# Nineteen pairs of projection units a layer as seven half-size products, gates through DRAM, units in 272 columns

## The chip, the cores and the metric

The kernel is one program on one core of a Trainium2 chip. The metric is the device time of one execution, in microseconds (us). The engines named below are TensorE (PE; its weight loads are PEld), VectorE (DVE), ScalarE (ACT), GpSimd (POOL) and SyncE (SP), which issues most of the DMAs.

## The reference, cut to what matters

Two layers of a trunk run over 1024 prompt tokens and 64 sample tokens (T = 1088 columns), with a model width of 1024. In each layer one projection of the normed input feeds four token mixers and the gates of the merge:

```python
h = rmsnorm(x, norm_w[l])
proj = h @ w_in[l]                       # 1024 -> 11,792 columns
(a_x, a_b, a_c, a_z, s_u, s_z, c_q, c_f, c_i, c_z,
 d_q, d_k, d_v, d_z, d_r, m_logit) = jnp.split(proj, pts, axis=-1)
...                                      # A short conv, B S5, C HGRN2, D GLA
branches = jnp.stack([y_a, y_b, y_c, y_d], axis=2)      # 512 channels each
p = jnp.einsum('blnw,nwd->blnd', branches, w_branch[l])
gates = jax.nn.sigmoid(m_logit.reshape(bsz, L, N_BRANCH, D_MODEL))
merged = jnp.sum(gates * p, axis=2)
x = x + merged @ w_out[l]
```

All of it is float32; the final output is normed once more.

## The kernel before

**Tiles.** Channels lie on the partitions and the 1088 tokens on the free axis. The normed input `h` is eight k-tiles of [128, 1088], each held as a high and a low part in float32r (`split`: ScalarE copies the high part, VectorE subtracts it). Weights come as tiles of [128, 4, 128] (four k-tiles by 128 output channels, 256 KB) and are split in the same way by `w_split`: `whi` by ScalarE, `wlo` by VectorE. A product is three matmuls: high x high, high x low, low x high.

**Units.** `unit(KT, xs)` makes 128 output channels for all tokens: for each k-tile, for each of the three parts, three matmuls of 384, 384 and 320 columns into one PSUM tile of three banks (`mm`, two such tiles). Projections have KT = 8; the branch outputs and the half-GLU have KT = 4. `tokens_unit` makes the values of the recurrences with the tokens on the partitions. The first two units of a layer (`lead_units`) take the tokens a third at a time.

**Order.** `ORDER` lists the units of a layer: S5 inputs (u), convolution (A: four units each), HGRN heads (H), GLA pairs (G), S5 outputs and half-GLU (U). `merge` follows: for each of four branches eight gate units (KT = 8, then a sigmoid by ScalarE) and eight branch units (KT = 4), with the product gate x branch on VectorE and the sum on GpSimd. `out_proj` closes the layer. Beside the stream of units run "lanes" (`Lane`, `pump`, `drain`): chains of small stages for the recurrences, S5 and setup, which are issued where a rough account of the engines (`Book`) finds their operands ready. `drain` issues what is left of a lane at once. `defer` holds small steps of which one is issued per k-step. Every engine's queue runs in the order of issue.

**Memory.** There are `NBIG` = 38 slots of [128, 1088]. `h` takes 16 of them from the lead units until the last gate unit of the merge. The lines of the profile all read L81: one helper (`Meter`) passes every instruction on, so rows are told apart by tile names (`mm` a unit's PSUM, `sm` a lane's).

## Time and profile before

| | |
|---|---|
| time, median of three runs | 3117.66 us (3117.42 to 3119.92) |
| the profiled execution: its span | 3116.5 us; the median of the runs is 1.2 us above it |
| TensorE busy | 3074.3 us in 19650 matmuls |
| VectorE, ScalarE, GpSimd busy | 1482.8, 969.4, 477.0 us |
| moved by DMA | 215.30 MB, 69 GB/s |
| instructions | 47347 |

The span is from the first to the last instruction. Busy time counts an engine's instructions where they overlap once only; a matmul's own duration overlaps with the next one's, so the cost of one in a stream is the step from one start to the next.

### The profile page before, as it was taken

The numbers are of one execution on the slowest core, as the hardware profiler recorded it, in microseconds if no ns is written. First come the engines' busy times: TensorE is split into PE (matmuls) and PEld (weight loads), VectorE is DVE, ScalarE is ACT, GpSimd is POOL, SyncE is SP. The second block draws the span as 40 slices with busy tenths as digits, with TensorE's granted clock in tenths as the row PEclk, the third lists the DMA queues.
The fourth block names the chain that finished last, engine by engine and source line by source line (L and its number), as shares of the span: only waits on it lengthen the run. The fifth ranks groups of instructions, "written<-read, shape, count | busy, mean of one in ns | idle before, by whom it ended". The sixth has DMA issues, their size and how long they took to land.

```text
span 3116.5 us, 47347 instructions
## 1 busy us (share of the span) xinstructions
PE 3074.3 (99%) x19650; PEld 2977.8 (96%) x19650; DVE 1482.8 (48%) x2670; ACT 969.4 (31%) x1769; POOL 477.0 (15%) x490
## 2 busy tenths in 40 slices
PE   8999999999999999999999999999999999999998
PEld 7999989999999999999899999999999999999997
DVE  4688665465641222116446885555565412221152
ACT  5223333425451212113331233334255412111221
POOL 2323011020210011103013411010202001111020
PEclk9999999999999999999999999999999999999999
DMA  4223122112331221213232221221113321212222
GB/s 133 71 69 95 36 59 75 36 36 62 82 110 44 73 73 45 73 45 98 85 90 82 75 71 58 60 64 36 39 54 80 113 73 45 73 48 70 58 85 88
DMA packets 260491, 215.30 MB, mean 69 GB/s; under 512 B 13984, under 2 KB 238000, under 8 KB 260276
## 3 DMA queue, kind: packets, MB, share of 16 engines
q1 hardware_dynamic: 251908, 185.14, 21.0%
q0 software_dynamic: 8368, 27.13, 2.7%
q8 instruction: 155, 2.54, 0.3%
q14 instruction: 60, 0.49, 0.1%
HBM read 168.14 MB, written 44.08 MB: 68 GB/s over the span
## 4 chain that ended last, share of the span: by engine, by line
PE 91%; DVE 4%; ACT 2%; issue 1%; POOL 1%; DMA 0%; SPq 0%; DVEq 0%; POOLq 0%; ACTq 0%
PE mm L81 79%; PE sm L81 12%; POOL mg L81 1%; ACT hi L81 0%; DVE att L81 0%; DVE wlo L81 0%; DVE g L81 0%; DVE prs L81 0%; DVE lo L81 0%; DVE H L81 0%; DVE w L81 0%; DVE pr L81 0%; DVE ya L81 0%; ACT L81 0%; ACT whi L81 0%
## 5 line engine op out<-in xcount | busy, mean ns | idle before, releaser
L81 DVE TENSOR_TENSOR wlo<-wraw,whi 128x512 fp32r<-128x512 f32 x400 | 298.5, 750 | 762.3 <-ACT whi L81 761.6
L81 PE MATMUL mm<-hi,wlo 128*128 128x384 f32 (+1 forms) x2592 | 580.7, 330 | 0.0
L81 PE MATMUL mm<-lo,whi 128*128 128x384 f32 (+1 forms) x2592 | 580.0, 330 | 0.0
L81 PE MATMUL mm<-hi,whi 128*128 128x384 f32 (+1 forms) x2592 | 576.7, 329 | 2.2 <-DVE g L81 1.0
L81 ACT ACTIVATE whi<-wraw 128x512 fp32r<-128x512 f32 x400 | 275.5, 692 | 741.8 <-PE mm L81 651.8
L81 PEld LDWEIGHTS mm<-hi,whi 128*128 128x128 f32 x2592 | 440.7, 188 | 5.5 <-issue 2.8
L81 PEld LDWEIGHTS mm<-hi,wlo 128*128 128x128 f32 x2592 | 442.3, 188 | 1.6 <-issue 1.3
L81 PEld LDWEIGHTS mm<-lo,whi 128*128 128x128 f32 x2592 | 441.0, 189 | 2.2 <-issue 1.6
L81 PE MATMUL mm<-xh,wlo 128*128 128x384 f32 (+1 forms) x1920 | 433.9, 331 | 1.2 <-DVE wlo L81 1.2
L81 PE MATMUL mm<-xh,whi 128*128 128x384 f32 (+1 forms) x1920 | 433.8, 331 | 1.0 <-ACT whi L81 0.8
L81 PE MATMUL mm<-xl,whi 128*128 128x384 f32 (+1 forms) x1920 | 433.1, 331 | 0.0
L81 PEld LDWEIGHTS mm<-xh,wlo 128*128 128x128 f32 x1920 | 328.3, 189 | 5.1 <-DVE wlo L81 2.8
L81 PEld LDWEIGHTS mm<-xh,whi 128*128 128x128 f32 x1920 | 328.1, 189 | 4.7 <-issue 1.9
L81 PEld LDWEIGHTS mm<-xl,whi 128*128 128x128 f32 x1920 | 327.8, 190 | 1.9 <-issue 1.5
L81 POOL TENSOR_TENSOR mg<-mg,g 128x1088 f32<-128x1088 f32 x46 | 136.8, 2974 | 1004.3 <-DVE g L81 974.2
L81 ACT ACTIVATE g<-mm 128x768 f32<-128x768 f32 (+1 forms) x128 | 72.9, 621 | 335.7 <-PE mm L81 335.7
L81 DVE TENSOR_TENSOR g<-g,mm 128x768 f32<-128x768 f32 x96 | 64.8, 716 | 122.3 <-PE mm L81 122.3
L81 ACT ACT_TABLE_LOAD x90 | 115.5, 1283 | 14.4 <-PE mm L81 12.1
L81 DVE COPY_PREDICATED att<-mask,sm 64x32 f32<-64x32 int32 (+9 forms) x184 | 93.7, 568 | 32.1 <-PE sm L81 31.8
L81 PE MATMUL mm<-hi,hi 128*128 128x512 f32 x256 | 79.3, 391 | 5.1 <-DVE g L81 3.2
L81 POOL DMA_DIRECT2D out_dram<-S x24 | 18.0, 751 | 430.2 <-DVE S L81 362.9
L81 PEld LDWEIGHTS sm<-q,k 128*64 128x64 f32 (+5 forms) x800 | 80.4, 172 | 2.9 <-issue 1.3
(332 smaller groups left out, 3996.9 us busy)
## 6 DMA issues: line engine op xcount, KB each, us to landing
wraw<-in_w_in_dram SPq DMA_DIRECT2D x328, 256.0 KB
y<-ysc SPq DMA_DIRECT2D x32, 544.0 KB
wraw<-in_w_branch_dram SPq DMA_DIRECT2D x64, 256.0 KB
ysc<-o POOLq DMA_DIRECT2D x16, 544.0 KB, 3.1
wo<-in_w_out_dram SPq DMA_DIRECT2D x16, 512.0 KB
out_dram<-S POOLq DMA_DIRECT2D x12, 512.0 KB, 4.6
usc<-u SPq DMA_DIRECT2D x8, 544.0 KB
ysc<-ya SPq DMA_DIRECT2D x8, 544.0 KB
```

The source lines that it names most:

```text
L81: r = fn(*a, **kw)
```

## The change

- 38 of a layer's 76 eight-tile units become 19 pairs (`PAIRED`): the convolution's (A: x with c, b with z), the S5 output gates (Z) and 18 of the 32 merge gates (M). A pair is a product of a 256-channel weight block with `h`, both cut in halves along the reduction, and the tokens cut in halves of 544: seven products of quarter blocks in place of eight (Strassen, in Winograd's form). `combine` makes the sums of quarters of `h` once a layer and splits them into high and low parts (16 slots); `prep` makes the sums of weight tiles on VectorE ahead of each split; `pair` runs the products and puts the results together out of PSUM on VectorE.
- All merge gates are computed ahead of the merge, the other 14 by `gate_unit`, stored to DRAM (`gsc`) and loaded by `merge`, which now has branch units alone, in the order 0, 2, 1, 3. The S5 output gates go through DRAM too (`szs`).
- Units run in two halves of 544 tokens, each two matmuls of 272 columns; `mm` is two banks in three buffers, and each half is emptied by itself (`out`).
- S5 of a layer (its loads too) starts after the pairs; the setup of S5 is drained after the third unit; the half-GLU's loads and gelus are issued beside the last GLA gate unit (`glu_begin`). Half of the merge's sums move from GpSimd to VectorE.
- Weight tiles have six buffers for raw loads, filled by `feed`, and the scratch of software-issued DMAs is 4096 bytes.

```diff
-ORDER = 'u0 u1 u2 u3 A0 A1 A2 H0 H1 H2 H3 G0 G1 A3 U'
+PAIRED = 'A0 M0 A1 M1 A2 M2 A3 M3 Z0 M4 Z1 M5 M6 M7 M8'
+EARLY = 'm18 m19'
+ORDER = 'm20 m21 m22 m23 m24 m25 m26 m27 m28 m29 m30 m31 H0 H1 H2 H3 G0 G1 U'
+BRANCHES = (0, 2, 1, 3)
+RAWS = 6
...
-        return self.ps.tile([128, 3, 512], F32, tag="mm", name=self.nm("mm"))
+        return self.ps.tile([128, 2, 512], F32, tag="mm", name=self.nm("mm"), bufs=3)
...
+    def feed(self):
+        while self.di in self.loaded:
+            self.di += 1
+        if self.nraw < RAWS:
+            self.w_dma(self.di)
+    def prep(self, j):
+        if j >= len(self.seq) or j in self.done:
             return
+        self.done.add(j)
         nc = self.nc
+        e, p = self.seq[j]
+        perm = self.plan[e][2]
+        drop = []
+        for i in range(e, e + (1 if p is None else 4)):
+            self.w_dma(i)
+        if p is None:
+            src = self.raws[e]
+            drop = [e]
+        else:
+            a11, a21, a22, a12 = (self.raws.get(e + i) for i in range(4))
+            new = lambda: self.wp.tile([128, 4, 128], F32, tag="wsum", name=self.nm("wsum"), bufs=2)
+            if p == 0:
+                src = a11
+            elif p == 1:
+                s1 = new()
+                src = new()
+                self.sums_[e] = s1, src
+                nc.vector.tensor_add(s1[:], a21[:], a22[:])
+                nc.vector.tensor_sub(src[:], s1[:], a11[:])
+            elif p == 2:
+                src = a12
+            elif p == 3:
+                src = self.sums_[e][0]
+            elif p == 4:
+                src = a21
+                nc.vector.tensor_sub(a21[:], a11[:], a21[:])
+                drop = [e, e + 1]
+            elif p == 5:
+                src = self.sums_.pop(e)[1]
+                nc.vector.tensor_sub(src[:], a12[:], src[:])
+                drop = [e + 3]
+            else:
+                src = a22
+                drop = [e + 2]
         hi = self.wp.tile([128, 4, 128], F32R, tag="whi", name=self.nm("whi"), bufs=4)
         lo = self.wp.tile([128, 4, 128], F32R, tag="wlo", name=self.nm("wlo"), bufs=4)
+        h, lv, r = hi[:], lo[:], src[:]
...
         nc.scalar.activation(h, r, AF.Copy)
         nc.vector.tensor_sub(lv, r, h.bitcast(F32))
+        for i in drop:
+            self.raws.pop(i)
+            self.nraw -= 1
+        self.ws[j] = (hi, lo)
+    def unit(self, KT, xs, out, last=False):
         nc = self.nc
+        j0, nw = self.wi, KT // 4
+        self.prep_to(j0 + nw)
+        ws = [self.ws.pop(j0 + i) for i in range(nw)]
+        self.wi += nw
+        for hb in range(2):
+            ps = self.mm()
+            for k in range(KT):
+                hi, lo = ws[k // 4]
+                xh, xl = xs[k]
+                terms = ((hi, xh), (hi, xl), (lo, xh))
+                for j, (wt, xt) in enumerate(terms):
+                    for b in range(2):
+                        s = HT * hb + HP * b
+                        nc.tensor.matmul(ps[:, b, :HP], wt[:, k % 4, :], xt[:, s:s + HP],
+                                         start=(k == 0 and j == 0), stop=(k == KT - 1 and j == len(terms) - 1))
+                    if j + 1 < len(terms):
+                        self.pump()
+                if k == 1:
+                    self.prep_to(self.wi + 1 + hb + (KT < 8))
+                if k % 4 == 2:
+                    self.feed()
+                if k % 2:
+                    self.step()
+                else:
                     self.pump()
+            out(ps[:, 0:2, :HP], (HT * hb, HT), 2)
+    def combine(self):
+        nc = self.nc
+        xs = [[None] * 4 for _ in range(4)]
+        f = {}
+        def full(i):
+            for n in (i, i + 4):
+                f[n] = self.big([128, T], name="xf")
+                (nc.gpsimd if n > 3 else nc.vector).tensor_add(f[n], self.h[n][0].bitcast(F32), self.h[n][1].bitcast(F32))
+        def sums(i):
+            a, b = f[i], f[i + 4]
+            t = self.big([128, 2, HT], name="xd")
+            f[i, 0] = t
+            nc.vector.tensor_sub(t[:, 1], b[:, HT:T], a[:, HT:T])
+            nc.vector.tensor_sub(t[:, 0], a[:, HT:T], a[:, 0:HT])
+            nc.vector.tensor_add(a[:, 0:HT], t[:, 1], a[:, 0:HT])
+            nc.vector.tensor_sub(b[:, 0:HT], b[:, 0:HT], a[:, 0:HT])
+        def split(i, n):
+            src = (f[i][:, 0:HT], f[i, 0][:, 0], f[i, 0][:, 1], f[i + 4][:, 0:HT])[n]
+            x = self.big([128, 2, HT], F32R, name="xc")
+            nc.scalar.activation(x[:, 0], src, AF.Copy)
+            nc.vector.tensor_sub(x[:, 1], src, x[:, 0].bitcast(F32))
+            xs[n][i] = (x[:, 0], x[:, 1])
+            if n == 3:
+                self.free(f[i], f[i + 4], f[i, 0])
+        self.h_sums = xs
+        for i in range(4):
+            self.defer.append(lambda i=i: full(i))
+            self.defer.append(lambda i=i: sums(i))
+            self.defer.append(lambda i=i: (split(i, 0), split(i, 1)))
+            self.defer.append(lambda i=i: (split(i, 2), split(i, 3)))
+    def quarters(self):
+        q = lambda k0, s: [tuple(x[:, s:s + HT] for x in self.h[k0 + k]) for k in range(4)]
+        t2, t1, t3, t4 = self.h_sums
+        return q(0, 0), t2, q(4, 0), t1, t3, q(4, HT), t4
+    def pair(self, out, a, b):
+        nc = self.nc
+        V = None
+        two = lambda x: x.rearrange("p (b n) -> p b n", b=2)
+        H1, H2 = slice(0, HT), slice(HT, T)
+        ops = self.quarters()
+        ps = {}
+        for p in range(7):
+            self.prep_to(self.wi + 1)
+            hi, lo = self.ws.pop(self.wi)
+            self.wi += 1
+            at, start = ((0, True), (1, True), (0, False), (2, True), (3, True), (2, False), (3, False))[p]
+            if start:
+                ps[at] = self.mm()
+            for k in range(4):
+                xh, xl = ops[p][k]
+                for j, (wt, xt) in enumerate(((hi, xh), (hi, xl), (lo, xh))):
+                    for c in range(2):
+                        nc.tensor.matmul(ps[at][:, c, :HP], wt[:, k, :], xt[:, HP * c:HP * c + HP],
+                                         start=(start and k == 0 and j == 0), stop=(k == 3 and j == 2),
+                                         skip_group_check=True)
+                    if j < 2:
+                        self.pump()
+                if k == 1:
+                    self.prep_to(self.wi + 3)
+                if k == 2:
+                    self.feed()
+                self.step()
+            v = ps[at][:, 0:2, :HP]
+            if p == 0:
+                V = self.big([128, HT], name="V")
+                nc.scalar.copy(two(V), v)
+            elif p == 1:
+                nc.vector.tensor_add(two(V), two(V), v)
+            elif p == 2:
+                out(0, v)
+            elif p == 3:
+                nc.vector.tensor_add(two(b[:, H2]), two(V), v)
+            elif p == 4:
+                nc.vector.tensor_add(two(b[:, H2]), two(b[:, H2]), v)
+            elif p == 5:
+                nc.vector.tensor_add(two(a[:, H2]), two(V), v)
+                out(1, None)
+            else:
+                nc.vector.tensor_add(two(b[:, H1]), two(V), v)
+                self.free(V)
+                out(2, None)
+    def pair_of(self, f, g, names=("pa", "pb")):
+        nc = self.nc
+        a, b = (self.big([128, T], name=n) for n in names)
+        two = lambda x: x.rearrange("p (b n) -> p b n", b=2)
+        def out(i, v):
+            if i == 0:
+                nc.scalar.activation(two(a[:, 0:HT]), v, f)
+            elif i == 1 and f != AF.Copy:
+                nc.scalar.activation(a[:, HT:T], a[:, HT:T], f)
+            elif i == 2 and g != AF.Copy:
+                nc.scalar.activation(b, b, g)
+        self.pair(out, a, b)
+        return a, b
...
+    def gate_unit(self, l, i):
+        g = self.big([128, T], name="g")
+        self.proj(l, "g", i, self.evac(g, AF.Sigmoid))
+        self.nc.sync.dma_start(self.gsc[l][i // 8][128 * (i % 8):128 * (i % 8) + 128, :], g)
+        self.free(g)
+    def gates_pair(self, l, j):
+        pair = self.pair_of(AF.Sigmoid, AF.Sigmoid, ("ga", "gb"))
+        for i, t in enumerate(pair):
+            d = 2 * (j % 4) + i
+            self.nc.sync.dma_start(self.gsc[l][j // 4][128 * d:128 * d + 128, :], t)
+            self.free(t)
+    def glu_begin(self, l):
...
+        for j in range(4):
+            load(j)
+        self.defer += [lambda: None] * YLAG
+        for j in range(4):
+            self.defer.append(lambda j=j: act(j))
...
+        u, ac = self.pair_of(AF.Copy, AF.Copy, ("au", "ac"))
+        nc.vector.tensor_mul(u, u, ac)
+        self.free(ac)
...
+        b, z = self.pair_of(AF.Copy, AF.Silu, ("ab", "az"))
+        nc.vector.tensor_mul(y, y, b)
         nc.vector.tensor_mul(y, y, z)
+        self.free(b)
...
+        units = [(n, d) for n in BRANCHES for d in range(8)]
+        g = {}
+        def gate(i):
+            if i < len(units):
+                n, d = units[i]
+                g[i] = self.big([128, T], name="g")
+                nc.sync.dma_start(g[i], self.gsc[l][n][128 * d:128 * d + 128, :])
+        def branch(i, y):
+            n, d = units[i]
+            gi = g.pop(i)
+            first = n == BRANCHES[0]
...
+            def out(p, span, nb):
+                gv = self.cut(gi, span, nb)
+                nc.vector.tensor_mul(self.cut(md, span, nb) if first else gv, gv, p)
+                if not first:
+                    s = slice(span[0], span[0] + span[1])
+                    (nc.vector if span[0] else nc.gpsimd).tensor_add(md[:, s], md[:, s], gi[:, s])
+            self.unit(4, y, out, last=(d == 7))
+            self.free(gi)
+        y = self.y
+        gate(0)
+        gate(1)
+        for i, (n, d) in enumerate(units):
+            b = i // 8
+            if d == 0 and b:
+                while self.defer:
+                    self.defer.pop(0)()
+                y = nxt
+            if d == 5 and b < 3:
+                if b == 2:
+                    self.drain(self.rec)
+                    self.drain(self.aux)
+                nxt = self.load_y(l, BRANCHES[b + 1])
+                self.defer += [lambda: None] * 4 + [lambda y=nxt, j=j: self.split(y, j) for j in range(4)]
...
+            gate(i + 2)
+            branch(i, y)
...
     def layer(self, l):
         if l:
-            self.s5l.q.append(self.s5_load(l))
             self.lead_units(l, lambda b, k: self.drain(self.aux) if b == 2 and k == 0 else None,
                             lambda b, k: self.step())
         self.aux.q.append(self.conv_begin(l))
+        if l:
+            self.keep = 0
+            self.combine()
+        self.u_unit(l, 2)
+        if l == 0:
+            self.drain(self.s5l)
+            self.keep = 0
+            self.combine()
+        self.u_unit(l, 3)
+        for op in EARLY.split():
+            self.gate_unit(l, int(op[1:]))
+        for op in PAIRED.split():
+            while self.defer:
+                self.defer.pop(0)()
+            self.drain(self.aux)
+            {"A": self.conv, "Z": self.z_pair, "M": self.gates_pair}[op[0]](l, int(op[1:]))
...
+        self.aux.q.append(self.conv_end(l))
+        self.s5l.q.append(self.s5_load(l))
         self.s5l.q.append(self.s5(l))
+        self.more = True
         for op in ORDER.split():
             i = int(op[1:] or 0)
-            if op[0] == "u":
-                if i > 1:
-                    self.u_unit(l, i)
-            elif op[0] == "A":
-                self.drain(self.aux)
-                self.conv(l, i)
-            elif op[0] == "H":
+            if op[0] == "H":
                 self.hgrn_units(l, i)
+            elif op[0] == "m":
+                self.gate_unit(l, i)
             elif op[0] == "G":
                 self.gla_units(l, i)
             else:
-                self.drain(self.tabs)
-                self.drain(self.s5l)
                 self.glu(l)
-        self.aux.q.append(self.conv_end(l))
...
+    nc = _bacc.Bacc("TRN2", target_bir_lowering=False, num_devices=1, dynamic_dma_scratch_size=4096)
```

## Rows read from the trace of the kernel before

**Rows 1.** The page: busy time of TensorE, and its granted clock in slices.
```profile
PE 3074.3 (99%) x19650; PEld 2977.8 (96%) x19650; DVE 1482.8 (48%) x2670; ACT 969.4 (31%) x1769; POOL 477.0 (15%) x490
...
PEclk9999999999999999999999999999999999999999
```

**Rows 2.** The page: the chain that ended last, by engine.
```profile
PE 91%; DVE 4%; ACT 2%; issue 1%; POOL 1%; DMA 0%; SPq 0%; DVEq 0%; POOLq 0%; ACTq 0%
```

**Rows 3.** The same chain in time (start us, us, what): longest piece.
```profile
2437.58 572.72 PE mm L81 x3450
```

**Rows 4.** Timeline of PE (start us, us), values unit: its longest wait.
```profile
398.65 0.58 PE L81 MATMUL mm<-whi,xh 128*128 128x256 f32 x1 [5.77 <-ACT v L81]
```

**Rows 5.** Windows (us, busy us of each engine, PEclk, DMA): wait, last recurrence.
```profile
392.50:399.00 6.50, 0.73 (x5) 0.52 (x4) 6.39 (x11) 2.71 (x12) 2.39 (x4) 0.73 0.12 49
399.00:406.00 7.00, 7.00 (x45) 6.61 (x45) 6.86 (x16) 2.65 (x14) 0.00 (x0) 0.76 0.01 2
...
741.00:896.00 155.00, 153.80 (x967) 147.46 (x966) 98.14 (x146) 85.34 (x106) 24.44 (x19) 0.98 0.27 73
```

**Rows 6.** Timeline of PE, wide values unit: two runs of 272 columns.
```profile
559.40 0.29 PE L81 MATMUL mm<-wideh,xl 128*128 128x272 f32 x1
...
561.77 0.29 PE L81 MATMUL mm<-widel,xh 128*128 128x272 f32 x1
...
564.14 0.29 PE L81 MATMUL mm<-wideh,xl 128*128 128x272 f32 x1
...
566.53 0.29 PE L81 MATMUL mm<-widel,xh 128*128 128x272 f32 x1
```

**Rows 7.** Timeline of PE: lead units' last third, third unit's start.
```profile
47.55 0.31 PE L81 MATMUL mm<-xl,whi 128*128 128x320 f32 x1
...
52.54 0.31 PE L81 MATMUL mm<-xh,wlo 128*128 128x320 f32 x1
53.06 0.76 PE L81 MATMUL mm<-xh,whi 128*128 128x384 f32 x3 [0.21 <-ACT u L81]
```

**Rows 8.** Groups of instructions by form, VectorE (busy us, mean ns).
```profile
L81 DVE TENSOR_TENSOR wlo<-wraw,whi 128x512 fp32r<-128x512 f32 x400 | 298.5, 750 | 762.3 <-ACT whi L81 761.6
...
L81 DVE TENSOR_TENSOR lo<-mg,hi 128x1088 fp32r<-128x1088 f32 x16 | 20.7, 1293 | 25.9 <-ACT hi L81 25.0
...
L81 DVE TENSOR_TENSOR yb<-sz,glu 128x1088 f32<-128x1088 f32 x8 | 18.4, 2306 | 21.2 <-POOL sz L81 21.2
...
L81 DVE TENSOR_TENSOR Tb<-f 128x544 f32<-128x544 f32 x12 | 8.6, 718 | 0.0
```

**Rows 9.** The same view, ScalarE.
```profile
L81 ACT ACTIVATE whi<-wraw 128x512 fp32r<-128x512 f32 x400 | 275.5, 692 | 741.8 <-PE mm L81 651.8 <-issue 73.1 <-DMA wraw<-in_w_in_dram 5.3
```

**Rows 10.** Timeline of VectorE, first and last of the setup of S5.
```profile
80.72 0.25 DVE L81 COPY prm<-sm 128x96 f32<-128x96 f32 x1
...
100.02 0.16 DVE L81 COPY Dcol<-sm 128x8 f32<-128x8 f32 x1
```

**Rows 11.** Timeline of ScalarE beside the first S5 gate units.
```profile
802.44 1.28 ACT L81 ACT_TABLE_LOAD   x1
803.74 1.12 ACT L81 ACTIVATE yv<-yv 128x1088 f32<-128x1088 f32 x1
804.89 1.11 ACT L81 ACTIVATE xh<-yv 128x1088 fp32r<-128x1088 f32 x1
...
808.16 1.28 ACT L81 ACT_TABLE_LOAD   x1
...
817.39 1.11 ACT L81 ACTIVATE xh<-yv 128x1088 fp32r<-128x1088 f32 x1
```

**Rows 12.** Windows: a stretch of the merge in which the DMA engines are full.
```profile
2695.00:2700.00 5.00, 5.00 (x32) 5.00 (x32) 0.00 (x0) 0.00 (x0) 0.00 (x0) 1.00 1.00 394
```

**Rows 13.** Timeline of ScalarE, the last GLA gate's evacuation.
```profile
740.21 1.14 ACT L81 ACTIVATE sz<-mm 128x768 f32<-128x768 f32 x2 [0.38 <-PE mm L81]
```

**Rows 14.** Timeline of GpSimd, the last recurrence's store.
```profile
895.47 0.53 POOL L81 DMA_DIRECT2D ysc<-o  x1 [13.93 <-ACT whi L81]
```

More of the change, by code (lines that the diff above doesn't have):

```diff
@@ L164, in __init__ @@
         self.inside = None
+        self.more = False
         self.u_done = 0
@@ L192, in fits @@
             return False
-        return not ln.need or len(self.alive) + ln.need <= NBIG - (ln.spare if self.rec.q else 0)
+        return not ln.need or len(self.alive) + ln.need <= NBIG - (ln.spare if self.rec.q or self.more else 0)
     def pump(self):
@@ L215, in force @@
     def force(self, lanes):
-        some = [x for x in lanes if x.q and self.fits(x)]
+        some = [x for x in lanes if x.q and self.fits(x)] or [
+            x for x in lanes if x.q and not (x.when and not x.when()) and len(self.alive) + x.need <= NBIG]
         assert some, [(x.need, len(x.q)) for x in lanes] + sorted(self.alive)
@@ L335, in tokens_unit @@
         i0 = self.wi
-        if not wide:
-            self.wi += 4
+        ws = []
         tail = self.tail(self.h)
-        for g in range(3):
+        for ts in ((0, 1), (2, 3), (4, 5), (8,), (6, 7)):
             ps = self.mm()
-            while g == 2 and self.defer:
+            while ts[0] == 8 and self.defer:
                 self.defer.pop(0)()
@@ L1441, in glu, with to_blocks, put @@
-    def glu(self, l):
+        out, end = self.u_evac(l, j)
+        self.proj(l, "s_u", j, out)
+        end()
+    def to_blocks(self, out, func):
+        def put(p, span, nb):
+            src = p.rearrange("p b (c s) -> p b c s", s=8) if nb > 1 else p.rearrange("p (c s) -> p c s", s=8)
+            dst = self.blocked(out, span, nb)
+            for b in range(nb):
+                self.nc.scalar.activation(dst[:, b] if nb > 1 else dst, src[:, b] if nb > 1 else src, func)
+        return put
@@ L1662, in branch @@
-            self.free(g)
-        y = load_y(0)
-        for n in range(3):
-            self.defer += [lambda: None] * 4 + [lambda y=y, j=j: split(y, j) for j in range(4)]
-            g = {}
-            for d in range(8 + LAG[n]):
-                if d < 8:
-                    g[d] = gate(n, d)
-                if d == 6 + LAG[n]:
-                    nxt = load_y(n + 1)
-                if d >= LAG[n]:
-                    branch(n, d - LAG[n], y, g.pop(d - LAG[n]))
-                    if n == 0 and d == DRAIN + LAG[n]:
-                        self.drain(self.rec)
-                        self.drain(self.aux)
-            y = nxt
```

380 lines of the change are left out of this document (168 added, 212 removed).

## The prediction

> **What bounds the kernel now.** I read the engines' busy times first [rows 1]. TensorE is busy for 99% of the span, and its granted clock is 0.9 or more of full speed in every fortieth. A busy TensorE is not one at its peak, so the chain that ended last was next [rows 2]: 91% of the span is TensorE, 4% VectorE, 2% ScalarE. The longest piece of that chain [rows 3] runs through the second merge without one break: 3450 matmuls in 572.72 us, 0.166 us each. Three such matmuls (384, 384 and 320 columns) are one "term" of a unit, a weight part against all 1088 tokens: 0.498 us. A projection unit has 8 x 3 = 24 terms, 11.95 us; a unit with four k-tiles has 12.
>
> So the kernel is bound by the number of columns that TensorE streams, and by hardly any wait. I went on to look for waits that exist all the same, since they show what a late operand costs. The worst [rows 4] is 5.77 us in a values unit, where TensorE waits for ScalarE to empty PSUM. The two windows from the wait on [rows 5] show the granted clock at 0.73 and 0.76 of full speed: a long wait is followed by a stretch at the lower level (1.2 GHz), and some 3 us more are lost.
>
> **The change, part by part. Pairs.** Per layer 38 of the 76 eight-tile units become 19 pairs. Before, a pair is 48 terms x 0.498 = 23.9 us. After, it is seven products of 4 k-tiles x 3 terms x 2 matmuls of 272 columns: 168 matmuls. The trace has that width in the values unit with the wide weights [rows 6]: the later run takes 19 steps in 2.39 us, 0.126 us each, every one with weights of its own. So 168 x 0.126 = 21.2 us, 2.7 us less a pair, and for 2 x 19 pairs **-104 us**.
>
> **272 columns elsewhere.** The other units issue four matmuls of 272 for three wider ones: 4 x 0.126 = 0.504 us a term for 0.498. A layer keeps 36 eight-tile units outside the lead (24 terms) and 36 four-tile ones (12): 1296 terms, 2592 in all, x 0.006 = **+16 us**. The price of one matmul carries much of the sum (some 16,750 of them: 1 ns is 17 us), so I bound it. From below: the earlier run of [rows 6] takes 19 steps in 2.37 us, 0.1247 each, 22 us less in all. From above: the 320-column matmuls of the lead units [rows 7] take 34 steps in 4.99 us, 0.1468 us; 48 columns fewer at 2.4 GHz are 0.020 us, which leaves 0.1268. The mean of a term's three, 0.166 for 362.7 columns, taken down by 90.7 columns in the same way, leaves 0.128, 37 us more. I take 0.126, the only row of that very width.
>
> A rule to weigh against this: the Trainium skill, TensorE: Matmul & The Clock Gate, section "Back-to-back issue gap", gives a matmul's columns at 2.4 GHz plus about 2.5 ns. By it a fourth matmul adds only those 2.5 ns to a term, and the extra term cost would be some 6 us and not 16; the rows show 12 to 15 ns above the columns, so I keep the rows.
>
> **VectorE and ScalarE in a pair.** Seven weight splits take 7 x 0.75 = 5.3 us of VectorE [rows 8], four sums of weight tiles some 0.7 each = 2.8, five sums out of PSUM of 544 columns 3.6 (0.72 each, an estimate by such a pass out of SBUF): 11.7 us. Where a sum comes ahead of a split, VectorE also waits for ScalarE's high part, 0.69 us [rows 9]: four times, 2.8 us. That is 14.5 of 21.2 us. The convolution adds about five passes over 1088 columns (1.29 us each [rows 8]) after its first pair: 21 us, just full. Splits run three products (9 us) ahead, and pairs without convolution lie between. I take 0.1 us a pair, **+4 us**; bounds 0 and 45 (16 convolution pairs at 24 us).
>
> **The first layer's start.** The setup of S5 is now drained after the third S5 unit, and sixteen steps of VectorE work (the combinations of h) follow before the first pair. Before, the setup's VectorE chain runs from 80.72 to 100.18 us [rows 10], beside units that don't need it; some 15 us of it are its own (19.5 less the weight splits between; an estimate). The combinations are 4 x 1.29 + 32 x 0.72 = 28 us, splits and masks 10 more: 53 us. The third unit starts at 53.06 us [rows 7], and four units give 48. I take **+8 us**, once; bounds 0 and 25. In the second layer the combinations start a unit earlier and no setup runs: nothing.
>
> **The half-GLU.** Before, ScalarE's four gelus and their splits run beside two S5 gate units, 24 us; the rows [rows 11] show them from 802.44 to 818.50, with a table load of 1.28 us each time the function goes from silu to gelu or back. Now the first gelu comes halfway through the last GLA gate unit, and the S5 gates are no longer there: 6 us of cover. The work is three table loads (3.9), one half's silu (0.65), two weight splits (1.4) and four times 2.2 us (8.8): 14.7 us, and 1.28 us for the last low part. The fourth input is there 22 us into a unit of 12.1; the first half of the next unit wants it at 14.4. So TensorE waits some 7.5 us, and by [rows 5] a lower clock follows for a while: 10 us a layer, **+20 us**. Bounds: 4 and 18 a layer. Of VectorE's work in these 24 us (two passes of 1.29 and 2.31 us [rows 8] for each of four tiles, splits, y's parts, 28 us) the excess is caught up in the first merge units, which need 2.2 us of 6.
>
> The Trainium skill, ScalarE: Activation LUTs, section "Table sets: the hidden batching unit", asks to do all calls of one set before the next; this order breaks that. It prices a switch at about 2.7 us with its drain, by which the wait would be some 4 us longer a layer; the rows show 1.28 us, after which the gelu starts at once.
>
> **S5's loads** are now issued when S5 starts and no longer a phase ahead. Some ten issues and a landing are exposed to the account that places the transposes: 2.5 us a layer, **+5 us**; bounds 0 and 8.
>
> **The gates through DRAM.** Stores of 557 KB lie beside the pairs, where two in 21 us are 53 GB/s. In the merge each unit of 6.05 us loads one gate, a weight tile of 262 KB and, in the last branch, 524 KB of the output weights: 222 GB/s. The queue moves 394 GB/s when full [rows 12], and a gate is issued two units (12 us) ahead. Behind the four tiles of y it may come 3 us late, with 6 us of PSUM in hand. Nothing; with that cover gone, 3 us at each of six bursts.
>
> **The last recurrence.** It ends 155 us after the last GLA gate's evacuation (740.21 to 895.47 [rows 13, 14]), under a convolution and S5's gates, with VectorE busy for 98 of these us [rows 5]. It now runs under the half-GLU (24 us) and 22 four-tile units (133 us), with the lane's own matmuls (an estimate of 27 us) between: 184 us. But of the 98 us some 46 were other work (20 splits 15, the convolution 12, the half-GLU's low parts and passes 19), which leaves the recurrence 52. Now the other work is 28 in the half-GLU, 2.2 and then 2.9 us for each of 8 and 14 merge units, and 11 for y's parts: 97. 52 + 97 = 149 of 184 us: it fits, with little to spare. **+6 us** for both layers; bounds 0 and 60.
>
> A third PSUM buffer for the units takes away part of the 5.77 us wait [rows 4]: **-3 us**.
>
> **Sum.** Against the profiled span of 3116.5 us: -104 + 16 + 4 + 8 + 20 + 5 + 6 - 3 = -48, that is 3068.5; the median of the runs is 1.2 us above the span, so **3070 us**.
>
> **The rivals.** *Almost no new wait.* The account places everything well, and only the two TensorE terms remain, with 5 to 10 us: 3037 us. For it speaks that the merge shows not one gap now. Against it: the gelus have to go somewhere.
> *A fixed cost per matmul, slower.* If the fixed part of a 272-column matmul is what the 384-wide ones show (1088 columns' terms, above) or more, TensorE's saving shrinks: at 0.128 us the time is 3105, at 0.129 it is 3122 and the gain is gone; at 0.130, 3138. Against it stand the rows of that width.
> *The recurrence is late.* VectorE is too full behind the half-GLU, and the drain ahead of the last branch waits 10 to 25 us a layer: 3090 to 3118.
> *VectorE bounds the convolution pairs.* Sixteen at 24 us: 3112.
>
> **How the numbers follow.** Forecast (3050 to 3092) 0.54; almost no new wait 0.21; recurrence late 0.12; VectorE in the pairs 0.05; fixed cost 0.08. The range leaves out the dearer half of the fixed-cost case and the best corner of the second: 3030 to 3114. About 0.2% (6 us) is what a measurement of this kernel can tell from no change. Faster: 0.54 + 0.21 + most of the late cases = 0.88; the same 0.05; slower 0.07.
>
> **What would show it.** Right: 272-column steps of 0.126 us in a pair and seven products in some 21 us; a gap of several us ahead of the first half-GLU unit of each layer, ended by ScalarE's high part, with a lower clock behind it; a merge without gaps. Wrong: steps of 0.128 us or more; gaps within the pairs ended by VectorE's low parts; waits for a gate's landing; a gap at the unit ahead of the last branch.

## The result, and the profile after

The changed kernel is slower, by 0.6%: 3138.24 us (median of 4 runs, 3133.99 to 3139.61) against 3118.11 (3117.42 to 3119.92), a ratio of 1.0061 [1.0047, 1.0075]. The forecast was 3070, with a range of 3030 to 3114. The profiled execution has a span of 3137.8 us.

The page of the kernel after: busy times, then TensorE by fortieths of the span with its granted clock (compare [rows 1]).

```profile
PE 2998.1 (96%) x23154; PEld 2901.2 (92%) x23154; DVE 1890.1 (60%) x3228; ACT 1109.5 (35%) x1881; POOL 445.4 (14%) x500
...
PE   8899999999999998899999999999999999979998
...
PEclk9999999999999999899999999999999999979999
```

TensorE is busy for 76 us less than before and the span is 21 us longer, so TensorE stands idle for some 97 us more. Two stretches show the two sides: one within the second layer's pairs, and the half-GLU and the start of the merge of the first layer (windows; the columns are those of [rows 5]).

```profile
1700.00:1900.00 200.00, 200.00 (x1610) 200.00 (x1609) 127.42 (x191) 68.56 (x102) 3.62 (x8) 1.00 0.26 77
...
1200.00:1225.00 25.00, 15.49 (x87) 13.67 (x87) 12.46 (x13) 24.53 (x25) 0.00 (x0) 0.73 0.41 148
1225.00:1250.00 25.00, 25.00 (x201) 24.92 (x200) 19.48 (x17) 13.99 (x19) 5.08 (x2) 1.00 0.30 82
1250.00:1275.00 25.00, 7.83 (x49) 7.61 (x49) 9.91 (x10) 0.63 (x1) 5.00 (x2) 0.66 0.77 226
```

In the pairs 1608 matmuls of 272 columns start in these 200 us (two of the 1610 counted started before), 0.1244 us each, and nothing waits. From 1200 to 1225 ScalarE is busy for 24.53 of 25 us and TensorE for 15.49. From 1250 to 1275 TensorE works 7.83 us, and the mean granted clock is 0.66 of full speed: behind the wait it is at the lower level (1.2 GHz).

To account for all of it I took from every step between two matmuls the mean undisturbed step of its form at full clock (the steps within a quarter of the form's median); what is over is waiting, or a matmul stretched by the lower clock.

| part | forecast | measured |
|---|---|---|
| TensorE's own steps (3014 to 2906) | -88 | -108 |
| first layer's start, 50 to 125 us | +8 | +24 |
| from there to the half-GLU, both layers | +6 | +21 |
| half-GLU, both | +20 | +28 |
| first units of the merge, both | 0 | +39 |
| rest of the merge and output projection | +6 | +15 |
| ahead of 50 us | 0 | +2 |

The sum is +21, as between the spans. The change does on TensorE more than I forecast, and loses 129 us to new waits and clock where I had 40: some 97 of them idle time, the rest mostly matmuls at the lower clock. The largest wait is the one that I had costed at nothing. TensorE, VectorE and SP's queue there (timelines; in brackets the idle time ahead of the instruction and what ended it; `g` is a gate loaded back from `gsc`, `mg` its product with a branch, `yb` VectorE's last pass over a tile of the half-GLU):

```profile
1269.14 0.82 PE L84 MATMUL mm<-hi,whi 128*128 128x272 f32 x2 [17.17 <-DVE mg L84]
...
1233.13 2.34 DVE L84 TENSOR_TENSOR yb<-sz,glu 128x1088 f32<-128x1088 f32 x1 [2.71 <-POOL sz L84]
...
1252.57 2.12 DVE L84 TENSOR_TENSOR yb<-sz,glu 128x1088 f32<-128x1088 f32 x1 [2.63 <-POOL sz L84]
1259.10 2.12 DVE L84 TENSOR_TENSOR yb<-sz,glu 128x1088 f32<-128x1088 f32 x1 [2.64 <-POOL sz L84]
1268.37 0.72 DVE L84 TENSOR_TENSOR mg<-g,mm 128x544 f32<-128x544 f32 x1 [7.15 <-DMA g<-gsc]
...
1261.24 0.53 SPq L84 DMA_DIRECT2D ysc<-yb  x1
1261.82 2.89 SPq L84 DMA_DIRECT2D g<-gsc  x3
```

The merge's first gates are issued on SP's queue behind the half-GLU's fourth store, which waits for the last yb pass (to 1261.22). Until a gate has landed no multiplication empties PSUM; TensorE fills the three buffers and stands for 17 us. The second layer repeats it (17.43).

The other new waits, in the same view. First TensorE in the first layer's start; then ScalarE, TensorE and VectorE in a pair of S5 gates; then TensorE ahead of the half-GLU, and part of what ScalarE does there.

```profile
91.23 0.82 PE L84 MATMUL mm<-xh,wlo 128*128 128x272 f32 x2 [5.52 <-DVE wlo L84]
98.45 0.62 PE L84 MATMUL mm<-xh,whi 128*128 128x272 f32 x2 [2.63 <-ACT whi L84]
...
391.48 1.28 ACT L84 ACT_TABLE_LOAD   x1
392.77 1.27 ACT L84 ACTIVATE sz<-mm 128x272 f32<-128x272 f32 x2
396.87 0.49 PE L84 MATMUL mm<-xh,whi 128*128 128x272 f32 x2 [2.60 <-DVE zb L84]
396.01 0.72 DVE L84 TENSOR_TENSOR zb<-V,mm 128x544 f32<-128x544 f32 x1
...
1207.87 0.68 PE L84 MATMUL mm<-xh,whi 128*128 128x272 f32 x2 [3.62 <-ACT xh L84]
1214.39 0.82 PE L84 MATMUL mm<-xh,whi 128*128 128x272 f32 x2 [3.92 <-ACT xh L84]
...
1203.14 1.11 ACT L84 ACTIVATE f<-f 128x1088 f32<-128x1088 f32 x1
1204.27 1.28 ACT L84 ACT_TABLE_LOAD   x1
1205.57 1.11 ACT L84 ACTIVATE yv<-yv 128x1088 f32<-128x1088 f32 x1
1206.71 1.11 ACT L84 ACTIVATE xh<-yv 128x1088 fp32r<-128x1088 f32 x1
1207.84 1.28 ACT L84 ACT_TABLE_LOAD   x1
```

The gelus (`yv`, with high parts `xh`) come right behind the last recurrence's gate functions (`f`), which my list of ScalarE's work in the half-GLU did not have.

### The profile page after: what moved, and what is told of

It is laid out like the page before. It is cut to its first block, busy times and chain, and to the rows that moved or that the text cites. A ratio compares the mean times of both kernels' runs of the same rounds, so it can differ in the third digit from the quotient of the medians.

```text
span 3137.8 us, 55699 instructions
## 1 busy us (share of the span) xinstructions
PE 2998.1 (96%) x23154; PEld 2901.2 (92%) x23154; DVE 1890.1 (60%) x3228; ACT 1109.5 (35%) x1881; POOL 445.4 (14%) x500
## 5 line engine op out<-in xcount | busy, mean ns | idle before, releaser
L84 PE MATMUL mm<-hi,whi 128*128 128x272 f32 (+1 forms) x2680 | 569.9, 293 | 48.8 <-DVE mg L84 35.9
L84 PE MATMUL mm<-hi,wlo 128*128 128x272 f32 (+1 forms) x2680 | 567.7, 293 | 0.0
L84 PE MATMUL mm<-lo,whi 128*128 128x272 f32 (+1 forms) x2680 | 567.3, 292 | 0.0
L84 PE MATMUL mm<-xh,whi 128*128 128x272 f32 (+1 forms) x1784 | 387.0, 297 | 28.7 <-ACT xh L84 15.1
L84 PE MATMUL mm<-xc,whi 128*128 128x272 f32 x2432 | 402.1, 287 | 0.0
L84 PE MATMUL mm<-xh,wlo 128*128 128x272 f32 (+1 forms) x1784 | 383.9, 295 | 8.8 <-DVE wlo L84 8.8
L84 PE MATMUL mm<-xl,whi 128*128 128x272 f32 (+1 forms) x1784 | 384.6, 296 | 3.8 <-DVE xl L84 3.8
L84 PEld LDWEIGHTS mm<-xc,whi 128*128 128x128 f32 x2432 | 341.3, 189 | 0.0
L84 PE MATMUL mm<-xc,wlo 128*128 128x272 f32 x1216 | 250.7, 288 | 0.0
L84 PEld LDWEIGHTS mm<-xc,wlo 128*128 128x128 f32 x1216 | 189.9, 188 | 0.0
```

The source lines that it names most:

```text
L84: r = fn(*a, **kw)
```

## The experiments

All times are medians; ratios are to the kernel before, which ran beside each experiment, at 3116.5 to 3118.3. "Below" is against the changed kernel's 3138.2 where nothing else is said. A ratio is known to some 0.15%, so that differences of under some 5 us (7, 9 and 10) are not clear of the spread; there the waits in the trace carry the reading, and not the time. The edits are shortened, and the comments in them are mine.

**1. The merge's gates first.**

```diff
+            if j == 2:                      # in glu, ahead of the third and fourth store
+                for d in range(2):
+                    t = self.big([128, T], name="g")
+                    nc.sync.dma_start(t, self.gsc[l][BRANCHES[0]][128 * d:128 * d + 128, :])
+                    self.first.append(t)    # merge takes these for its first two units
```

> The changed kernel with one edit: the loads of the merge's first two gates are issued on SP's queue ahead of the half-GLU's third and fourth stores, not behind them. Theory 'queue': the 17.3 and 17.6 us waits at the start of the merges are the order of SP's queue alone, so both go to under 2 us and the time falls by some 32 us, to about 3106. Rival 'VectorE': the merge's first multiplication also stands behind the last yb pass on VectorE itself (it ends at 1261.22, seven us before the first multiplication starts), so each wait only shrinks to about 10 us, and the time falls by some 15 us, to about 3123.

3119.2 us, 1.0005 [0.9996, 1.0014] of before: 19 below. TensorE and VectorE at the merge's start:

```profile
1260.71 0.82 PE L84 MATMUL mm<-hi,whi 128*128 128x272 f32 x2 [9.81 <-DVE mg L84]
...
1257.99 2.12 DVE L84 TENSOR_TENSOR yb<-sz,glu 128x1088 f32<-128x1088 f32 x1 [2.64 <-POOL sz L84]
1259.95 0.71 DVE L84 TENSOR_TENSOR mg<-g,mm 128x544 f32<-128x544 f32 x1
```

The multiplication now follows the last yb pass with no idle time. The queue is about half of the wait (8.5 us stay in the second layer); the rest is VectorE's, as the rival had it.

**2. The stores on GpSimd's queue.**

```diff
-            nc.sync.dma_start(self.ysc[l][1][...], yt)
+            if j: store(j - 1, held)        # nc.gpsimd.dma_start; the fourth behind the loop
```

> The changed kernel with one edit: the half-GLU's four stores are issued on GpSimd's queue, each one tile later, so that SP's queue holds only loads there. Theory 'queue': also the chain of the four tiles is held up by SP (the loads of the third and fourth gate of S5 stand behind the stores of the first and second tile), so the last yb pass ends some 10 us earlier, and the waits at the merge's start fall from 17 to under 4 us: about 3108. Rival 'VectorE': the chain's pace is set by VectorE's and GpSimd's own passes and by the recurrence's work between them; the last yb pass ends where it did, some 10 us of each wait stay, about 3123.

3121.7, 1.0013 [1.0003, 1.0022]. The waits at the merges' start are 9.9 us, the last yb pass starts at 1256.67 (1259.10 in the changed kernel, 1257.99 in the first experiment), 2.4 us earlier where the theory asked some 10: the stores do not set the chain's pace. The rival again.

**3. The gelus a unit earlier.**

```diff
-            if pr == 1 and hh == 1:
+            if pr == 1 and hh == 0:
                 self.more = False
                 self.glu_begin(l)
```

> The changed kernel with one edit: the half-GLU's inputs and gelus start one projection unit (12 us) earlier, ahead of the last GLA gate unit but one. Theory 'gelus': the waits ahead of the half-GLU's first unit (11 us a layer) and the lower clock behind them (10 us in the first layer) are ScalarE's gelus coming late; they vanish, and the time falls by 25 to 35 us, to about 3108. Rival 'moved': the gelus take the same ScalarE time and three table loads from the evacuations of the unit that they now lie beside, so a wait of 4 to 8 us a layer comes there, and the gain is 10 us or less; the wait at the start of the merge grows by what is won here if its end is set by the gates' loads and not by TensorE (then no gain at all).

3144.3, 1.009 [1.0073, 1.0107], 6 slower than the changed kernel. The wait has moved (TensorE, and ScalarE ahead of it):

```profile
1228.31 0.82 PE L84 MATMUL mm<-xh,whi 128*128 128x272 f32 x2 [9.03 <-ACT glu L84]
...
1222.78 1.28 ACT L84 ACT_TABLE_LOAD   x1
1224.12 1.11 ACT L84 ACTIVATE f<-f 128x1088 f32<-128x1088 f32 x1
1225.13 1.09 ACT L84 ACTIVATE hi<-y 128x1088 fp32r<-128x1088 f32 x1
1226.24 1.28 ACT L84 ACT_TABLE_LOAD   x1
1227.54 0.72 ACT L84 ACTIVATE glu<-mm,cols 128x544 f32<-128x544 f32 x1
```

The functions of the recurrence come behind the gelus now, and hold up the evacuation of the half-GLU itself.

**4. No pairs.**

```diff
     def pair(self, out, a, b):
+        self.unit(8, self.h, c(a))          # c: evacuation by a copy
+        out(0, a[:, 0:HT].rearrange("p (b n) -> p b n", b=2)); out(1, None)
+        self.unit(8, self.h, c(b))
+        out(2, None)
```

> The changed kernel with the seven-product pairs alone undone: each pair is two ordinary units of 272 columns (192 matmuls for 168), evacuated by a copy and the same functions after it; the combinations of h are still made, and everything else stands. Theory 'TensorE': a pair of 21.0 us becomes 23.8 us, 38 times: 106 us slower, about 3244. Rival 'the pairs give it back': their VectorE sums cost waits elsewhere, and undoing them costs 60 us or less, under 3200.

3236.67, 1.0384 [1.0363, 1.0405]: 98.4 slower. On TensorE 38 x 24 matmuls of 0.1244 us are 113, so the pairs cost some 15 elsewhere. The pairs themselves are worth about what the forecast said (104, less 4 for VectorE).

**5. GpSimd's adds ahead of the units,** with the first experiment's edit.

```diff
+            gs = self.big([128, T], name="gs")           # ahead of the tile's unit
+            nc.gpsimd.tensor_add(gs, sg[j][0].bitcast(F32), sg[j][1].bitcast(F32))
...
-            nc.gpsimd.tensor_add(sz, sg[j][0].bitcast(F32), sg[j][1].bitcast(F32))
-            nc.vector.tensor_mul(yn, v3(sz), v3(g))
+            nc.vector.tensor_mul(yn, v3(gs), v3(g))
```

> The first experiment's edit (the merge's first two gates loaded ahead of the half-GLU's last stores), and one more: GpSimd's add of each tile's two parts writes a buffer of its own and is issued ahead of the tile's unit, not after VectorE's first pass. Theory 'serial chain': each tile costs 1.3 us on VectorE, then 2.5 us on GpSimd while VectorE is idle, then 2.3 us on VectorE; without the stop between, the last yb pass ends 8 to 10 us sooner, the 10.0 and 8.5 us waits that the first experiment left go to under 2 us, and the time is some 16 us below the first experiment's 3119, about 3103. Rival 'VectorE is full': the recurrence's parts and the splits of y and of the weights fill the gaps, over 6 us of each wait stay, about 3113 or more.

3110.85, 0.9986 [0.9975, 0.9998]: 8 below the first experiment, half of what the theory asked. VectorE, behind the last yb pass, and its window (third pair of numbers):

```profile
1252.38 2.26 DVE L84 TENSOR_TENSOR yb<-gs,glu 128x1088 f32<-128x1088 f32 x1
1254.49 0.80 DVE L84 TENSOR_TENSOR att<-sm,ident 128x512 f32<-128x512 f32 x2
...
1261.47 0.71 DVE L84 TENSOR_TENSOR mg<-g,mm 128x544 f32<-128x544 f32 x1
...
1225.00:1250.00 25.00, 23.27 (x182) 22.82 (x181) 24.66 (x19) 10.92 (x15) 10.04 (x2) 1.00 0.47 128
```

The yb passes end at 1254.6 and not 1260.1, but seven us of the recurrence's parts follow ahead of the multiplication; the wait is still 8.1 us (10.0 in the first experiment). VectorE is full: 24.66 of 25 us. On the wait the rival was right; the 8 us that were won lie later. The same stretch of the merge in the first experiment, then in this one:

```profile
1300.00:1400.00 100.00, 97.22 (x741) 92.40 (x740) 75.35 (x122) 27.62 (x45) 29.16 (x24) 0.95 0.39 132
```

```profile
1300.00:1400.00 100.00, 100.00 (x799) 96.52 (x798) 73.69 (x112) 30.46 (x49) 27.56 (x22) 1.00 0.46 152
```

TensorE makes 58 matmuls more in these 100 us.

**6. Gate units behind GLA, taken from S5's cover.**

```diff
-ORDER = 'm20 ... m31 H0 H1 H2 H3 G0 G1 U'
+ORDER = 'm20 ... m29 H0 H1 H2 H3 G0 G1 m30 m31 U'   # glu_begin ahead of m30
```

> The changed kernel with one edit: the last two gate units of each layer stand behind the last GLA unit, and the half-GLU's inputs and gelus start ahead of them, so that two eight-tile units lie beside them, as in the kernel before. Theory 'cover': the waits ahead of the half-GLU (11 us a layer, and 10 us of lower clock behind them) go to under 2 us, and the last recurrence gets 24 us more: about 3108, 30 us less than the changed kernel. Rival 'moved': S5 loses 24 us of its cover, and the waits at the first values unit (5.5 us) grow by as much as is won, or the last recurrence's own functions on ScalarE still hold up an evacuation by some 9 us a layer, as in the third experiment: 3125 or more.

3294.19, 1.0569 [1.0553, 1.0585], 156 slower. Neither theory had that size. S5's late stages (`H`) fall among the units of the later heads, where TensorE waits for them in place, and waits in the recurrences grow with them (`prh`). One matmul of S5 in the changed kernel, then the same in this one, with the longest wait:

```profile
656.76 0.50 PE L84 MATMUL sm<-H,gt 128*128 128x136 f32 x2 [0.95 <-DVE H L84]
```

```profile
1013.74 0.82 PE L84 MATMUL sm<-H,gt 128*128 128x136 f32 x2 [12.78 <-DVE H L84]
1249.80 0.80 PE L84 MATMUL sm<-prh,ones_r 128*128 128x512 f32 x1 [18.05 <-DVE prh L84]
```

**7. S5 gates' first quarter by a copy.**

```diff
             if i == 0:
-                self.to_blocks(sz[0], AF.Silu)(v, (0, HT), 2)
+                self.nc.scalar.copy(a[:, 0:HT].rearrange("p (b n) -> p b n", b=2), v)
             elif i == 1:
-                self.to_blocks(sz[0], AF.Silu)(a[:, HT:T], (HT, HT), 1)
+                self.to_blocks(sz[0], AF.Silu)(a, (0, T), 1)
```

> The changed kernel with one edit: in the two pairs of S5 gates a layer, the first finished quarter is evacuated by a plain copy, and its silu comes with the rest of the tile, half a pair later. Theory 'table load': the 2.76 us wait in each of the four such pairs comes from the silu's table load and two strided evacuations, which stand ahead of a weight's high part on ScalarE, and so ahead of VectorE's read of a partial product that TensorE goes on to accumulate on: all four go, 11 us, about 3127. Rival 'tight anyway': VectorE has only one product (3.0 us) for that read, and another wait of the same size takes its place: no change, 3136 or more.

3133.31, 1.0052 [1.0037, 1.0067]: 5 below. TensorE's first wait in such a pair:

```profile
394.05 0.49 PE L84 MATMUL mm<-xh,whi 128*128 128x272 f32 x2 [0.83 <-DVE zb L84]
```

The first wait falls from 2.60 to 0.83 us, but a new one of 1.23 us came in the next pair, ended by ScalarE's copy of that pair's first product (`V`), which stands behind a silu of 2.39 us:

```profile
407.46 0.53 PE L84 MATMUL mm<-xh,whi 128*128 128x272 f32 x2 [1.23 <-ACT V L84]
```

By the account above 3 of the 12 us around these four pairs came back: the theory is right on the first wait, the rival on what took its place.

**8. A later start, with units taken from S5's cover.**

```diff
-EARLY = 'm18 m19'
+EARLY = ('m18 m19 m20 m21', 'm18 m19')     # by layer; ORDER of layer 0 begins at m22
...
+        self.u_unit(l, 3)                  # ahead of the drain and combine in layer 0
```

> The changed kernel with one edit, in the first layer only: the setup of S5 and the combinations of h come behind the fourth S5 unit, not the third, and four gate units and not two lie between them and the first pair. Theory 'VectorE's setup': the waits between 50 and 120 us (16 us, and 9 us of lower clock) come from some 64 us of VectorE work ahead of the first pair beside 48 us of units; with 72 us of units they go to under 5 us: about 3116. Rival 'borrowed': the two units are missing as cover for S5 later in this layer, where the waits at the values units (5.5 and 6.0 us) grow, and the gain is under 8 us.

3194.1, 1.0255 [1.0234, 1.0275], 56 slower. The start gained some 12 us by the account; S5's late stages fell out of place as in the sixth, in this layer alone. Both experiments leave S5 ten gate units of twelve; whether free buffers or the account of the engines then sends its stages so far back was not separated.

```profile
1025.04 0.82 PE L84 MATMUL sm<-H,gt 128*128 128x136 f32 x2 [12.52 <-DVE H L84]
```

**9. One pair a layer unpaired, behind GLA** (S5 keeps its twelve units).

```diff
-PAIRED = '... M6 M7 M8'
-ORDER = 'm20 ... G0 G1 U'
+PAIRED = '... M6 M7'
+ORDER = 'm20 ... G0 G1 m16 m17 U'           # glu_begin ahead of m16
```

> The changed kernel; in each layer one pair of gates is made two ordinary units again, which stand behind the last GLA unit, with the half-GLU's inputs and gelus started ahead of them. Unlike the sixth experiment S5 keeps all its twelve gate units, and its transposes stand in TensorE's order where they do in the changed kernel. Theory 'cover': a pair undone costs 2.8 us a layer, the 21 us at the half-GLU (waits and lower clock) go, and the last recurrence gets 24 us more ahead of the merge: about 3105, 30 us or more below the changed kernel. Rival 'ScalarE': the gelus and the last recurrence's own functions still hold up evacuations by some 9 us a layer, as in the third experiment: 3125 or more. Had the sixth experiment lost its time to the units behind GLA themselves, and not to S5, this one would lose as much: over 3200.

3134.79, 1.0059 [1.0043, 1.0075]: 3.5 below, no change clear of the spread. S5 stays in its place, and the loss of the sixth is gone: it was S5's. But TensorE waits within the last recurrence:

```profile
1203.26 0.31 PE L84 MATMUL sm<-prh,ones_r 128*64 128x64 f32 x1 [12.24 <-DVE att L84]
1210.40 1.45 PE L84 MATMUL sm<-prs,ones_r 128*128 128x512 f32 x2 [4.65 <-DVE prs L84]
```

**10. One pair of the first layer unpaired, ahead of the pairs.**

```diff
+PAIRED = ('... M6 M7', '... M6 M7 M8')      # by layer
+EARLY = ('m18 m19 m16 m17', 'm18 m19')      # drain and combine behind u3 in layer 0
```

> The changed kernel; in the first layer alone one pair of gates is made two ordinary units again, which stand ahead of the first pair, and the setup of S5 and the combinations come behind the fourth S5 unit. S5 keeps its twelve gate units. Theory 'VectorE's setup': of the 25 us lost between 50 and 120 us some 12 to 18 come back, for 2.8: about 3125. Rival: the combinations follow the setup as closely as before on VectorE, and the waits only move behind it: no change, 3135 or more. Had the eighth experiment lost its time at the start, this one would be slower by 50 us too.

3133.61, 1.0055 [1.0036, 1.0074]: 4.6 below, with the 2.8 paid. By the account the start loses 11 us less, so the waits there have the cause that the theory named; the time shows under half of its size.

**11. All that gained, together** (1, 5, 7, 9, 10).

> All edits that gained, together: the merge's first gates loaded ahead, GpSimd's adds early, the S5 gates' first quarter copied, one pair a layer unpaired behind the GLA units, and one more in the first layer ahead of the pairs (three pairs in all undone, 8 us). Theory 'separate waits': the gains add up: 27 us of the fifth experiment, 5 of the seventh, 30 of the ninth of which some 10 are the same waits, 12 of the tenth: about 3075, 1.4% below the kernel before. Rival 'VectorE uncovers the next': with TensorE no longer waiting in the half-GLU, the yb passes and the recurrence's parts come as late against the merge as now, and over half of the gains at the half-GLU and the merge's start is the same time counted twice: 3095 or more.

3113.79, 0.9993 [0.9983, 1.0002]. The rival: not faster than the fifth. What holds up the last recurrence's sums is seen here (TensorE, then VectorE):

```profile
1197.84 0.31 PE L84 MATMUL sm<-prh,ones_r 128*64 128x64 f32 x1 [12.77 <-DVE att L84]
...
1193.75 1.29 DVE L84 TENSOR_TENSOR xl<-yv,xh 128x1088 fp32r<-128x1088 f32 x1 [2.87 <-ACT xh L84]
1195.89 1.29 DVE L84 TENSOR_TENSOR xl<-yv,xh 128x1088 fp32r<-128x1088 f32 x1 [0.85 <-ACT xh L84]
1197.10 1.41 DVE L84 TENSOR_TENSOR att<-sm,ident 128x512 f32<-128x512 f32 x3
```

VectorE is idle, waiting for a gelu's high part (xh); behind that low part stands the read of the sums that TensorE needs. VectorE's order, not its work, is the wait.

**12. The same with the gelus seven steps later.**

```diff
-YLAG = 3
+YLAG = 10
```

> The eleventh experiment's kernel with one number changed: the four gelus start ten steps behind the loads of their inputs, not three, so they lie beside the second of the two gate units behind GLA. In the eleventh, TensorE waited 21 us a layer within the last recurrence's sums, because VectorE's reads of them stood behind the gelus' low parts. Theory 'queue order': these waits go, with the lower clock behind them, and no other of the size comes: 40 to 55 us less than the eleventh, 3060 to 3075. Rival 'ScalarE is full': the same ScalarE work then comes ahead of the half-GLU's first unit, with waits of 10 us a layer or more there: 3090 or more.

3081.87 (3078.07 to 3082.93), 0.9891 [0.9877, 0.9906]: 32 below the eleventh, and 1.1% faster than the kernel before. TensorE's waits at the half-GLU, and its windows (to be held against those of after):

```profile
1196.27 0.52 PE L84 MATMUL mm<-xl,whi 128*128 128x272 f32 x2 [2.19 <-DVE xl L84]
1199.21 0.82 PE L84 MATMUL mm<-xh,whi 128*128 128x272 f32 x2 [2.18 <-ACT xh L84]
...
1200.00:1225.00 25.00, 22.35 (x153) 21.43 (x153) 22.73 (x25) 13.25 (x17) 12.38 (x5) 0.84 0.66 223
1225.00:1250.00 25.00, 21.40 (x160) 21.02 (x160) 24.36 (x30) 4.39 (x8) 3.46 (x3) 0.93 0.60 180
```

The recurrence's waits for its sums are gone, some 5 us of short ones came ahead of the half-GLU, and 5 us are left at a later stage of the recurrence within it, of which this is the longer:

```profile
1234.62 1.33 PE L84 MATMUL sm<-apad,k 128*120 128x128 f32 x8 [3.38 <-DVE att L84]
```

The merge starts without a gap. By the account above, waits and clock fall from 217 us in the changed kernel to 147, for 8.8 us more of TensorE's steps. The time lies between the theory's 3075 and the rival's 3090.

**13. Gelus at the start of the second GLA pair** (the edits of 5, 7, 10; glu_begin in gla_units ahead of d_q).

> The fifth, seventh and tenth experiments' edits together, and the half-GLU's inputs and gelus started at the beginning of the second GLA pair's units, some 60 us earlier than in the changed kernel. Theory 'queue order': ScalarE has idle time there, so the gelus cost nothing, and the wait ahead of the half-GLU goes: 25 us or more below the fourteenth run. Rival 'ScalarE is full' or 'buffers': eight more SBUF buffers are held through the last 60 us of units, so stages of the recurrence before are forced early in TensorE's order (79 of its matmuls in a stretch where there were 28), and the waits move there: within 10 us of the fourteenth run, or slower.

3149.53, 1.0104 [1.0085, 1.0123], 54 slower than the next. The recurrence before comes early in TensorE's order, where it waits for VectorE (3.91 us for `att` at 1099.04 is the longest wait there): the rival's outcome. That the buffers force it early is argued from the code; no run separates it.

**14. The edits of 5, 7 and 10, gelus unmoved.**

> The fifth, seventh and tenth experiments' edits together (gates first, adds early, S5 gates' quarter copied, one pair of the first layer unpaired ahead of the pairs), with the gelus where the changed kernel has them. Theory 'separate waits': 3110.9 less 5 and less 4.5: about 3101, 0.5% below the kernel before. Rival: the tenth's shift of S5 and of the recurrences in the first layer costs the fifth's gain there: 3108 or more.

3095.6, 0.9933 [0.9912, 0.9953]: the gains of waits that lie far apart add up. That it is 5 us better than their sum of 3101 is within the runs' spread (3091.15 to 3104.65).

## Why the prediction was wrong

**TensorE's terms were right in kind and too small.** I took 0.126 us for 272 columns, the later of the two runs of that width [rows 6]; undisturbed steps are 0.1244 in the pairs and 0.1249 elsewhere, nearer to the earlier run, my bound from below. With some 17,000 of them the sum is -108 and not -88: the term "272 columns elsewhere" is some +5, and a pair takes 20.9 us. The rule that I weighed against the rows, in the Trainium skill, TensorE: Matmul & The Clock Gate, section "Back-to-back issue gap", is given there for an isolated matmul and not for a stream; here the steps stay 11 ns above the columns. The rival of a dearer matmul is refuted, and that its time of 3138 at 0.130 us is the one that came is chance. The fourth experiment shows the pairs' worth by itself.

**The step that failed most: "The gates through DRAM: nothing".** I argued with bandwidth and with two units of lead. The lead is an order on a queue: the loads' issue stood behind four stores, each waiting for VectorE. Experiment 1 shows the queue (about half of 17 us) and that the rest is VectorE's own order. Experiment 5 shows that GpSimd's part in the chain of four tiles is little of this rest: the recurrence's parts take its place. In 11 and 12, with two units more behind GLA, the wait is gone, in 11 at the price of waits within the recurrence's sums. I had priced this cover, if gone, at 3 us; it was 17.2 and 17.4, and the clock fell with it: 39 us in all. A wait for a gate's landing was my own sign of being wrong, and a slower kernel had 0.07.

**The half-GLU** had its mechanism right (a gap ended by ScalarE's high part, a lower clock behind) and its size low: 28 for 20. Missing were the last recurrence's gate functions, which stand ahead of the gelus with table loads of their own. The rule of batching by set that I had weighed, from the Trainium skill, ScalarE: Activation LUTs, section "Table sets: the hidden batching unit", bears on this more than I allowed: the trace has six loads of 1.28 us between 1201.8 and 1225.9 us, 7.7 of ScalarE's 24 us. ScalarE was not full for good: with two units of cover and the gelus behind the recurrence's parts (12) the work fits, but for some 5 us of waits.

**The first layer's start**: the mechanism as forecast, 24 us where I took 8 of a bound of 25. The sum of VectorE's work was there, at 53 us for 48 of units; VectorE is busy for 62.4 us from 53 us to the first pair at 131.3, so the sum was low and the choice within the bounds too kind.

**The last recurrence** "fits, with little to spare": the engine's total fits, its order does not. The stretch behind the merge's first units lost 15 us more than before where I had 6. By the account it holds 23 us of waits and clock in both layers, 19 in experiment 1, 5 in experiment 5 and 3 in experiment 12: it goes with the edit of experiment 5, which takes VectorE's stops out of the half-GLU. A gap ahead of the last branch, my sign of a late recurrence, is there, but short (2.52 us). Which of the waits in that stretch is whose was not separated.

**VectorE in the pairs** cost nothing but in S5's gates, 11 us, by a silu and its table load ahead of a weight's high part on ScalarE (7): not the cause that my +4 stood for. Of the remaining 10 us between the start and the half-GLU, the values units' waits of 5 to 6 us (three after, one before [rows 4]) are the main part; no experiment tried them. The -3 for a third PSUM buffer did not come: that wait is still there. What S5's loads cost, +5 in the sum, was not separated.

## What to carry to other kernels

When work is taken off the engine that bounds a kernel, re-count what that work was hiding: here 108 us came off TensorE, and 129 us of waits and lower clock came for it. Cost a prefetch by what stands ahead of it on its in-order queue, up to the last wait of those instructions, and not by its bandwidth; do the same for each engine's own queue, since 7 steps' difference in where four gelus stand was 32 us. Cover has owners: two units moved from beside S5 to where they seemed to be missing cost 156 us (6), while two pairs undone for the same purpose cost nothing that could be told from the spread (9), and with the gelus placed right are part of the fastest kernel (12).

## What the runs showed of the hardware

A matmul of 272 columns with weights of its own keeps to 0.1244 us over 1608 in a row, less than the 0.126 of the unit with wide weights before. In this kernel a partial sum that VectorE reads in the middle of an accumulation leaves it only the time of the product between, 3.0 us: a silu with its table load of 1.28 us on another engine was enough to break it, and 2.6 us of waiting came (experiment 7 moves both and takes the first wait to 0.83).
